# Three blocks of expert 0 ahead of the mixture of experts, four small blocks behind it, and routing in another order

## The chip, the cores and the metric

The kernel runs on one core of a Trainium2 chip. A core has TensorE (PE, matrix products; PEld is its weight load), VectorE (DVE), ScalarE (ACT), GpSimd (POOL) and SyncE (SP), which here only issues transfers; 16 DMA engines move the data between HBM and the on-chip memory. Each engine takes its instructions in order, and semaphores order the engines among each other. The metric is the time on the device of one execution, in microseconds (us), median of three runs.

## The reference

A trunk of two layers over 256 tokens of width 1024, in float32. The first layer (gating and pooling, then a dense SwiGLU) and the second layer's mixer (short convolution and latent attention) are not touched. The change lies at the end of the second layer's mixer, in the routing of its mixture of experts, and in the order of the experts' work:

```
x = x + g_m * mix
h = rmsnorm(x, norm_ffn_w) * (1 + sc_f) + sh_f
logits = h @ router_w                       # 256 tokens x 8 experts
top_v, top_i = top_k(logits, 2)             # two experts for each token
gates = softmax(top_v) put at top_i
y = sum over e of gates[:, e] * swiglu(h, w_gu[e], w_down[e])   # w_gu 1024 x 7168, w_down 3584 x 1024
out = x + g_f * y
```

All weights of all eight experts are read: 8 x 42 MiB, 336 transfers of 1 MiB.

## The kernel before

**Experts by place.** Routing counts the tokens of each expert. Expert 0 always has place 0. The other seven are put into places 1 to 7 by their counts, on the chip; places 1, 3 and 5 hold 128 tokens ("L"), places 0, 2, 4, 6 and 7 hold 64 ("S"). Which expert has a place from 1 up is known only when `Route.rest` has written `index` (L459); SP loads it into a register (L1519, in `Work.__init__`) and forms the addresses of that place's weights from it. Expert 0's addresses are known at compile time.

**Blocks.** The work of a place is cut into 7 blocks of 512 hidden columns. A block has four "up" chunks (1 MiB of `mgu` each) and two "down" chunks (1 MiB of `mdn` each). An S block multiplies the raw float32 weights (L1469 up, L1489 down). An L block first splits each chunk into a high and a low float32r part (ACT copy L113, DVE subtraction L116), and makes three products of them (L295, L297, L301). There are 35 S blocks and 21 L blocks. The list `blocks` mixes them: 2 S blocks (both of expert 0), then L blocks with the other S blocks spread between them, then 2 S blocks. In `seq` the up chunks of a block come before the down chunks of the block ahead of it. `run` emits one chunk of `seq`; `after(n, f)` puts a step n chunks later; `part_next` loads and splits an L chunk three L chunks ahead.

**Buffers.** A raw chunk lies in one of 14 buffers, taken in turn: `ring` (5), `keep` (8) and `extra` (1). An S chunk's buffer is free when PE has used it, an L chunk's when it has been split. `keep` and `extra` lie in memory that earlier phases give back; `extra` comes when the dense part is closed. All transfers are issued by SP.

**Orders.** The instructions of PE, ACT, DVE and POOL stand in program order from the end of the mixer on (`manual_schedule`). Those of SP are not in that set; a scheduler may put a transfer ahead of another.

**From the mixer to the experts.** `Close` finishes the mixer: `products(i, n)` are PE's last products for token half i and column half n, `add` the residual (DVE), `square` and `rstd` the norm (ACT, DVE, POOL). `flip` turns 512 columns of x (PE, copied by ACT), `use` multiplies them by the router (L1262). `Route.top2(i)` finds the two best experts of half i on DVE, `place(i)` counts positions within each expert by a product with a triangular matrix (L422, L425). `Gather.rows(i)` makes a selection matrix for half i (DVE, P and Q), `pick64(i)` applies it (PE L1363), `part64` scales the result into `hgS` (ACT and DVE); then the first up chunk of expert 0 can run. `gate_row` turns the last gate g_f into rows (8 transposes, L200). `rest` computes the softmax gates, the counts, the order of the experts, `index` and `over` (whether a place overflows).

**The end.** After the last S block `scatter2_front` multiplies the sum by g_f (L1494), `scatter2_back` spreads it to the tokens (PE L1501), adds it (DVE L1401) and stores four pieces of 256 KB (L1506, all from SP).

The order around the change, in the kernel before:

```python
cur = Gather(slots_of(stat, 0), 64, 4)
grows = [gate_row(1, 5, n, psa()) for n in range(2)]
cur.rows(0); route.top2(1); cur.pick64(0)
grow = gate_copy(pool, grows)
route.place(1); cur.rows(1); cur.pick64(1); cur.part64()
for n, ev in enumerate(seq):
    run(ev)
    if n == 1:
        placed, index, most, over = route.rest(pool, ranks, caps)
        ...
    if n == 5:
        gather_steps(1)
    if 7 <= n < 7 + AHEAD:
        part_next()
```

Of the kernel before, what the change touches and what calls it, by code (L numbers as in the profile page):

```python
# [7 lines left out]
F32 = mybir.dt.float32  # L8
# [13 lines left out]
NE = 8  # L22
# [20 lines left out]
def trunk_kernel(ctx, tc, x_in, c_in, pos_in, cols_in, rows_in,  # L43
# [345 lines left out]
    class Route:  # L389
# [12 lines left out]

        def top2(self, i, between=None):
            lg, m1, m2, f, oh1, oh2 = (t[:, i, :] for t in (self.lg, self.m1, self.m2, self.f, self.oh1, self.oh2))
            i1, i2, l2, maskb = (t[:, i, :] for t in (self.i1, self.i2, self.l2, self.maskb))
            vec.scalar_tensor_tensor(lg, self.lgp[i][:, :NE], self.ss[i][:, 3:4], shR, OP.mult, OP.add)
            vec.max_with_indices(m1, i1, lg)
            vec.tensor_copy(f[:, 0:1], i1[:, 0:1])
            vec.tensor_scalar(oh1, iota[:, :NE], f[:, 0:1], None, op0=OP.is_equal)
            vec.scalar_tensor_tensor(l2, oh1, -3.0e38, lg, OP.mult, OP.add)  # L410
            if between:
                between()
            vec.max_with_indices(m2, i2, l2)
            vec.tensor_copy(f[:, 1:2], i2[:, 0:1])
            vec.tensor_scalar(oh2, iota[:, :NE], f[:, 1:2], None, op0=OP.is_equal)
            vec.tensor_tensor(maskb, oh1, oh2, OP.add)
            vec.tensor_tensor(self.mask[:, i, :], oh1, oh2, OP.add)
# [8 lines left out]

        def rest(self, pool, ranks, caps):

# [9 lines left out]
            vec.tensor_tensor(self.gates, oh1, oh2, OP.add)  # L438
            ps = pst()
            pe.matmul(ps[:, 0:8], onesb, self.maskb[:, 0, :], start=True, stop=False)  # L440
            pe.matmul(ps[:, 0:8], onesb, self.maskb[:, 1, :], start=False, stop=True)
            vec.tensor_copy(self.count, ps[:, 0:8])

# [8 lines left out]
            vec.tensor_tensor(more, rank[:, None, :].to_broadcast([128, NE, NE]),  # L452
                              ranks[:, :, None].to_broadcast([128, NE, NE]), OP.is_equal)
            prod, placed = pool.tile([128, 8, NE, NE], F32, tag="w2", name="prod"), pl(8, NE)
            vec.tensor_tensor(prod, stat[:, :, None, :].to_broadcast([128, 8, NE, NE]),
                              more[:, None, :, :].to_broadcast([128, 8, NE, NE]), OP.mult)
            vec.tensor_reduce(placed, prod, AX.X, OP.add)
            index = pool.tile([128, NE], I32, name="index")
            vec.tensor_copy(index, placed[:, 7, :])  # L459

            above, most = pl(NE), pl(2)
# [406 lines left out]
    with Phase("mix1_late", w4=3, w2=2) as late, ExitStack() as early:  # L868
# [415 lines left out]
        flip(0, 1)  # L1284
        cl_.products(1, 1)
        cl_.add(1, 0)
        cl_.square(1, 0)
        use(0, 0)
        use(0, 1)
        flip(1, 0)  # L1290
        use(1, 0)
        cl_.add(1, 1)
        flip(1, 1)
        cl_.square(1, 1)
        route.top2(0, lambda: cl_.rstd(1))
        use(1, 1)
        route.place(0)
        early.close()
# [6 lines left out]
    shcol = mods[:, 1, 24:32]  # L1305
    with Phase("experts", w4=1, w2=2, aTL=1, hgH=1, hgL=1, hgS=1, P=1, Q=1, PT=3) as pool:
        sm = pool
# [184 lines left out]
        def scatter2_front(o):  # L1492
            og = sm.tile([128, 512], F32, tag="w2", name=nm("og"))
            vec.tensor_tensor(og, o, grow2, OP.mult)  # L1494
            return og

        def scatter2_back(gcol, og, g_, last=False):
            for i in range(2):
# [3 lines left out]
                for h in range(2):  # L1502
                    sl = slice(h * 512, (h + 1) * 512)
                    add_rows(i, h, ps[h], gcol[i])
                    if last:
                        sp.dma_start(out[i * 128:(i + 1) * 128, sl], ys[i][:, sl])  # L1506

# [21 lines left out]
        streams = {k: [(k, p, j) for p in range(NE) if (CAPS[p] == 128) == (k == "L") for j in range(7)] for k in "SL"}  # L1529
        blocks, nS, nL = [], len(streams["S"]), len(streams["L"])  # L1530
        for n in range(nL):
            while len(blocks) - n < 2 + (nS - 2) * n // nL:
                blocks.append(streams["S"][len(blocks) - n])
            blocks.append(streams["L"][n])
# [9 lines left out]
        parted = [ev for ev in seq if ev[0][0] == "L"]  # L1544
        AHEAD = 3
        halves, work, later = [], {}, []
# [108 lines left out]
        cur = Gather(slots_of(stat, 0), 64, 4)  # L1655
        grows = [gate_row(1, 5, n, psa()) for n in range(2)]
        cur.rows(0)
        route.top2(1)
        cur.pick64(0)
        grow = gate_copy(pool, grows)  # L1660
        route.place(1)
        cur.rows(1)
        cur.pick64(1)
        cur.part64()
        work[0] = Work(0, stat)
        work[0].g = cur
        for n, ev in enumerate(seq):
            run(ev)
            if n == 1:
                placed, index, most, over = route.rest(pool, ranks, caps)  # L1670
                cur.back()
                grow2 = pool.tile([128, 512], F32, name="grow2")
                for h in range(2):
                    act.copy(grow2[HALF[h]], grow[HALF[h], h * 512:(h + 1) * 512])
            if n == 5:
                gather_steps(1)
            if 7 <= n < 7 + AHEAD:
                part_next()
# [93 lines left out]
```

## Time and profile before

| | |
|---|---|
| median of 3 runs | 1303.78 us (1303.51 to 1304.12) |
| profiled execution, whole | 1305.34 us |
| its span, first to last instruction | 1303.5 us |
| mean granted TensorE clock | 0.973 of full |
| busy in the span: PE, DVE, ACT, POOL | 93%, 57%, 39%, 8% |
| DMA over the span | 358 GB/s |

Busy shares are of the span. A matmul's end is modelled, so a busy PE is not PE at its peak. The granted clock is 1.0 at 2.4 GHz and 0.5 at 1.2 GHz. Times of the trace count from the first instruction; the experts' first product starts at 444.78 us, the last one ends near 1292.5 us.

### The profile page before, as it was taken

What the parts mean: (1) busy time and instruction counts of PE and PEld (TensorE: products, weight loads), DVE (VectorE), ACT (ScalarE), POOL (GpSimd) and SP (SyncE); (2) the same over time, 40 slices, a digit from 0 to 9 for tenths busy, and PEclk for the clock granted to TensorE, in tenths of its full rate; (3) what the DMA queues carried; (4) which work ended last, traced back from release to release, by engine and by line L of the source; (5) the groups of instructions that cost most, each with busy time, mean ns of one, the idle gap of its engine ahead of it and who ended that gap; (6) DMA issues with size and microseconds to landing.
All of it is one profiled execution on the core that took longest, in us unless ns stands there. A gap on an engine that the chain in (4) does not pass through costs nothing.

```text
span 1303.5 us, 18766 instructions
## 1 busy us (share of the span) xinstructions
PE 1215.1 (93%) x7175; PEld 872.9 (67%) x7175; DVE 745.5 (57%) x1085; ACT 510.6 (39%) x768; POOL 108.3 (8%) x130
## 2 busy tenths in 40 slices
PE   1996999998999999999999999999999999999996
PEld 0575999997988766565565576665656666756663
DVE  3879898887786464353454445454535553544532
ACT  1044444345753254343353244343422353424420
POOL 2773000002171000000000000000000000000000
PEclk9997999999999799999999999999998999999999
DMA  6887888894667099999999998999999999999995
GB/s 264 341 315 293 285 351 329 322 358 163 225 220 266 10 421 421 418 420 419 419 420 418 419 419 348 419 419 419 420 418 421 403 394 419 419 418 419 419 419 203
DMA packets 65477, 466.47 MB, mean 358 GB/s; under 512 B 7522, under 2 KB 7650, under 8 KB 9315
## 3 DMA queue, kind: packets, MB, share of 16 engines
q1 hardware_dynamic: 65380, 465.20, 88.7%
q8 instruction: 58, 0.95, 0.3%
q14 instruction: 39, 0.32, 0.1%
HBM read 464.12 MB, written 1.05 MB: 357 GB/s over the span
## 4 chain that ended last, share of the span: by engine, by line
PE 69%; DMA 18%; DVE 7%; issue 2%; POOL 2%; ACT 2%; SPq 0%; DVEq 0%; POOLq 0%; ACTq 0%
PE gu L1469 14%; DMA raw<-in_mgu 13%; PE o L1489 7%; DMA raw<-in_mdn 5%; PE pb L314 3%; PE pb L313 3%; PE pb L316 3%; PE o L295 3%; PE o L297 3%; PE o L301 2%; PE g L295 2%; PE pa L599 2%; DVE junk L539 2%; PE u L295 2%; PE g L297 2%
## 5 line engine op out<-in xcount | busy, mean ns | idle before, releaser
L116 DVE TENSOR_TENSOR L<-raw,H 128x1024 fp32r<-128x1024 f32 x347 | 412.4, 1222 | 165.3 <-PE u L301 66.2
L113 ACT CAST H<-raw 128x1024 fp32r<-128x1024 f32 x350 | 350.7, 1046 | 119.8 <-PE u L297 80.1
L1469 PE MATMUL gu<-raw,hgS 128*64 128x256 f32 x2240 | 260.8, 386 | 10.3 <-DMA raw<-in_mgu 10.2
L1469 PEld LDWEIGHTS gu<-raw,hgS 128*64 128x64 f32 x2240 | 156.7, 138 | 105.8 <-DMA raw<-in_mgu 20.8
L1489 PE MATMUL o<-raw,aS 128*64 128x512 f32 x560 | 131.9, 605 | 1.7 <-DMA raw<-in_mdn 1.3
L539 DVE SCALAR_TENSOR_TENSOR junk<-raw,cact 128x1024 bf16<-128x1024 f32 x96 | 123.0, 1303 | 7.7 <-DMA raw<-in_ada 7.6
L1475 DVE TENSOR_TENSOR msg<-msg,gu 128x256 f32<-128x256 f32 x35 | 14.7, 421 | 192.7 <-ACT msg L1474 192.6
L313 PE MATMUL pb<-hH,H 128*128 128x256 f32 x432 | 106.3, 284 | 0.3 <-ACT cb L999 0.3
L314 PE MATMUL pb<-hL,H 128*128 128x256 f32 x432 | 106.0, 283 | 0.0
L1474 ACT ACTIVATE msg<-gu 128x256 f32<-128x256 f32 x35 | 13.4, 384 | 233.5 <-PE gu L1469 233.4
L313 PEld LDWEIGHTS pb<-hH,H 128*128 128x128 f32 x432 | 82.3, 190 | 1.1 <-ACT cb L999 0.6
L1489 PEld LDWEIGHTS o<-raw,aS 128*64 128x64 f32 x560 | 37.2, 138 | 68.1 <-issue 61.9
L314 PEld LDWEIGHTS pb<-hL,H 128*128 128x128 f32 x432 | 82.4, 191 | 0.4
L295 PE MATMUL g<-H,hgH 128*128 128x512 f32 x168 | 68.9, 410 | 0.0
L295 PE MATMUL u<-H,hgH 128*128 128x512 f32 x168 | 67.4, 401 | 0.0
L297 PE MATMUL g<-H,hgL 128*128 128x512 f32 x168 | 67.3, 401 | 0.0
L297 PE MATMUL u<-H,hgL 128*128 128x512 f32 x168 | 66.9, 398 | 0.0
L301 PE MATMUL u<-L,hgH 128*128 128x512 f32 x168 | 66.5, 396 | 0.0
L301 PE MATMUL g<-L,hgH 128*128 128x512 f32 x168 | 66.4, 395 | 0.0
L316 PE MATMUL pb<-hH,L 128*128 128x256 f32 x432 | 59.7, 280 | 0.0
L295 PE MATMUL o<-H,aTH 128*128 128x512 f32 x168 | 56.6, 418 | 0.0
L316 PEld LDWEIGHTS pb<-hH,L 128*128 128x128 f32 x432 | 54.9, 189 | 0.0
(396 smaller groups left out, 1528.1 us busy)
## 6 DMA issues: line engine op xcount, KB each, us to landing
raw<-in_mgu SPq DMA_DIRECT2D x224, 1024.0 KB, 19.8
raw<-in_mdn SPq DMA_DIRECT2D x112, 1024.0 KB, 19.8
raw<-in_ada SPq DMA_DIRECT2D x48, 1024.0 KB, 6.0
raw<-in_fgu SPq DMA_DIRECT2D x22, 1024.0 KB, 6.7
raw<-in_fdn SPq DMA_DIRECT2D x11, 1024.0 KB, 6.6
raw<-in_oin_c SPq DMA_DIRECT2D x6, 1024.0 KB, 5.1
raw<-in_ein_vp SPq DMA_DIRECT2D x4, 1024.0 KB, 7.8
raw<-in_eout SPq DMA_DIRECT2D x4, 1024.0 KB, 7.7
```

Of the source, the lines that this page charges most:

```text
L113: act.copy(self.to(q), raw[:, q * self.f:(q + 1) * self.f])
L116: eng.tensor_tensor(self.to(q), raw[:, q * self.f:(q + 1) * self.f], high.half(q).bitcast(F32), OP.subtract)
L295: pe.matmul(o, xH(k, i), wH(k, n), start=first and m == 0, stop=False)
L297: pe.matmul(o, xL(k, i), wH(k, n), start=False, stop=False)
L301: pe.matmul(o, xH(k, i), wL(k, n), start=False, stop=last and m == len(ks) - 1)
L313: pe.matmul(o, wH(k), hH[:, k, :], start=(k == 0), stop=False)
L314: pe.matmul(o, wH(k), hL[:, k, :], start=False, stop=False)
L316: pe.matmul(o, wL(k), hH[:, k, :], start=False, stop=(k == KD - 1))
L539: vec.scalar_tensor_tensor(junk, raw[:, a * D:(a + 1) * D], 1.0, cact, OP.mult, OP.mult, accum_out=mods[:, l, j + a:j + a + 1])
L599: pe.matmul(vp[part][i], h0[:, k, i * 128:(i + 1) * 128], w[:, kk * D + part * 512:kk * D + (part + 1) * 512], start=(k == 0), stop=(k == 7))
L1469: pe.matmul(gu[HALF[h], n * 256:(n + 1) * 256], g_.full[:, k, :], w[:, lo:lo + 256], start=(k == 0 and n == 0), stop=(k == KD - 1), skip_g ...
L1489: pe.matmul(o[HALF[h]], a[:, kk, c, :], w[:, kk * D + h * 512:kk * D + (h + 1) * 512], start=(j == 0 and c == 0 and kk == 0), stop=(j == 6 ...
```

## The change

1. **Blocks.** `LEAD` is 3: three S blocks of expert 0 stand ahead of the first L block (places 0.0, 0.1, 0.2), and four S blocks stand behind the last one. The L chunks begin to be loaded three chunks ahead of the first L chunk, that is at chunks 13 to 15 of `seq` in place of 7 to 9, and expert 1's gather begins at chunk 11 in place of 5.
2. **Routing.** `rest` is split: `counts` (two small products and a copy) runs before `pick64(1)`; `order` (the order of the experts, and of the table by place at first only the rows for count and index) runs behind the first chunk in place of the second; `gate` (the softmax gates) and the other six rows of the table come behind `index`.
3. **End of the mixer.** `products(1, 1)` is cut in two halves, the second behind `flip(1, 0)`; `top2(0)` and `place(0)` run whole before `add(1, 1)`, `flip(1, 1)`, `square(1, 1)` and `rstd(1)`, where `top2(0)` was interrupted for `rstd(1)`.
4. **Gate rows.** `gate_row` and its copies move behind chunks 1 and 2 of `seq`; the copy `grow2` goes, and `scatter2_front` multiplies two halves of 64 partitions by two instructions.
5. **Stores.** Of the four stores at the end SP issues two and ACT two.
6. A fourth buffer for `PT`.

```diff
-        def top2(self, i, between=None):
+        def top2(self, i):
...
-            if between:
-                between()
...
-        def rest(self, pool, ranks, caps):
+        def counts(self):
+            ps = psb("ps")
+            for i in range(2):
+                pe.matmul(ps[:, 0:8], onesb, self.maskb[:, i, :], start=(i == 0), stop=(i == 1))
+            vec.tensor_copy(self.count, ps[:, 0:8])
+
+        def gate(self):
...
-            ps = pst()
-            pe.matmul(ps[:, 0:8], onesb, self.maskb[:, 0, :], start=True, stop=False)
-            pe.matmul(ps[:, 0:8], onesb, self.maskb[:, 1, :], start=False, stop=True)
-            vec.tensor_copy(self.count, ps[:, 0:8])
+
+        def order(self, pool, ranks, caps):
...
-            vec.tensor_tensor(prod, stat[:, :, None, :].to_broadcast([128, 8, NE, NE]),
-                              more[:, None, :, :].to_broadcast([128, 8, NE, NE]), OP.mult)
-            vec.tensor_reduce(placed, prod, AX.X, OP.add)
-            index = pool.tile([128, NE], I32, name="index")
+
+            def by_place(lo, hi):
+                vec.tensor_tensor(prod[:, lo:hi], stat[:, lo:hi, None, :].to_broadcast([128, hi - lo, NE, NE]),
+                                  more[:, None, :, :].to_broadcast([128, hi - lo, NE, NE]), OP.mult)
+                vec.tensor_reduce(placed[:, lo:hi, :], prod[:, lo:hi], AX.X, OP.add)
+            by_place(6, 8)
             vec.tensor_copy(index, placed[:, 7, :])
-
+            self.gate()
+            by_place(0, 6)
...
-        cl_.products(1, 1)
+        cl_.products(1, 1, (0,))
         cl_.add(1, 0)
         cl_.square(1, 0)
         use(0, 0)
         use(0, 1)
         flip(1, 0)
+        cl_.products(1, 1, (1,))
+        route.top2(0)
         use(1, 0)
+        route.place(0)
         cl_.add(1, 1)
         flip(1, 1)
         cl_.square(1, 1)
-        route.top2(0, lambda: cl_.rstd(1))
+        cl_.rstd(1)
         use(1, 1)
-        route.place(0)
...
-            vec.tensor_tensor(og, o, grow2, OP.mult)
+            for h in range(2):
+                vec.tensor_tensor(og[HALF[h]], o[HALF[h]], grow[HALF[h], h * 512:(h + 1) * 512], OP.mult)
...
-                        sp.dma_start(out[i * 128:(i + 1) * 128, sl], ys[i][:, sl])
+                        (sp, act)[h].dma_start(out[i * 128:(i + 1) * 128, sl], ys[i][:, sl])
...
+        LEAD = 3
         for n in range(nL):
-            while len(blocks) - n < 2 + (nS - 2) * n // nL:
+            while len(blocks) - n < LEAD + (nS - LEAD - 2) * n // nL:
...
-        AHEAD = 3
+        AHEAD, FIRST = 3, seq.index(("LU", 1, 0, 0))
...
-        grows = [gate_row(1, 5, n, psa()) for n in range(2)]
         cur.rows(0)
+        cur.pick64(0)
         route.top2(1)
-        cur.pick64(0)
-        grow = gate_copy(pool, grows)
         route.place(1)
         cur.rows(1)
+        route.counts()
         cur.pick64(1)
...
+            if n == 0:
+                placed, index, most, over = route.order(pool, ranks, caps)
+                cur.back()
             if n == 1:
-                placed, index, most, over = route.rest(pool, ranks, caps)
-                cur.back()
-                grow2 = pool.tile([128, 512], F32, name="grow2")
-                for h in range(2):
-                    act.copy(grow2[HALF[h]], grow[HALF[h], h * 512:(h + 1) * 512])
-            if n == 5:
+                grows = [gate_row(1, 5, m, psb()) for m in range(2)]
+            if n == 2:
+                grow = gate_copy(pool, grows)
+            if n == FIRST - 5:
                 gather_steps(1)
-            if 7 <= n < 7 + AHEAD:
+            if FIRST - 3 <= n < FIRST - 3 + AHEAD:
                 part_next()
```

## Rows read from the trace of the kernel before

**Rows 1.** Page, part 2: busy tenths of the DMA engines, 40 slices of 32.6 us

```profile
DMA  6887888894667099999999998999999999999995
```

**Rows 2.** Waits of SP's queue, 416 to 456 us: us in total, times, longest

```profile
SPq L1519 <- DVE pl L466: 37.6, 1, 37.6
```

**Rows 3.** Transfers issued from 380 to 432 us: count, size, us to landing

```profile
raw<-in_mgu SPq DMA_DIRECT2D x8, 1024.0 KB, 7.0
...
raw<-in_mdn SPq DMA_DIRECT2D x1, 1024.0 KB, 4.8
```

**Rows 4.** Windows: length, busy by engine, granted clock, DMA share, GB/s

```profile
422.00:424.00 2.00, 2.00 (x14) 1.77 (x13) 0.99 (x3) 0.94 (x3) 0.55 (x1) 1.00 0.68 287
424.00:426.00 2.00, 2.00 (x10) 1.58 (x9) 0.55 (x1) 1.37 (x4) 0.00 (x0) 1.00 0.00 0
...
480.00:500.00 20.00, 18.35 (x114) 10.59 (x113) 7.43 (x8) 7.26 (x10) 0.00 (x0) 1.00 1.01 419
```

**Rows 5.** Timeline, 434 to 454 us: start, us, engine, line, operation

```profile
434.74 1.95 PE L200 MATMUL pa<-ident,mods 128*128 128x128 f32 x8
...
436.56 3.65 PE L1363 MATMUL pt<-Q,x 128*128 128x64 f32 x16
...
441.17 3.68 PE L1363 MATMUL pt<-Q,x 128*128 128x64 f32 x16 [0.93 <-DVE Q L1337]
...
444.78 4.76 PE L1469 MATMUL gu<-raw,hgS 128*64 128x256 f32 x32
...
449.91 0.17 DVE L447 SCALAR_TENSOR_TENSOR pl<-stat,iota 128x8 f32<-128x8 f32 x1
...
452.53 0.17 DVE L459 CAST index<-pl 128x8 int32<-128x8 f32 x1
...
453.75 0.36 SPq L86 DMA_DIRECT2D raw<-in_mgu  x1
```

**Rows 6.** Waits of PE, 455 to 600 us

```profile
PE gu L1469 <- DMA raw<-in_mgu: 6.6, 13, 0.6
PE o L1489 <- DMA raw<-in_mdn: 0.6, 1, 0.6
```

**Rows 7.** Waits of PE, 455 us to the end

```profile
PE gu L1469 <- DMA raw<-in_mgu: 10.2, 20, 0.6
...
PE o L1489 <- DMA raw<-in_mdn: 1.3, 2, 0.6
```

**Rows 8.** Timeline of PE: two down chunks and four up chunks, S blocks

```profile
837.36 3.65 PE L1489 MATMUL o<-raw,aS 128*64 128x512 f32 x16
...
841.53 7.13 PE L1469 MATMUL gu<-raw,hgS 128*64 128x256 f32 x64
```

**Rows 9.** A window of the middle, and the stretch ahead of the experts

```profile
800.00:820.00 20.00, 19.16 (x132) 12.17 (x132) 7.97 (x9) 4.75 (x6) 0.00 (x0) 1.00 0.75 299
...
430.00:447.00 17.00, 15.34 (x74) 13.53 (x75) 7.03 (x38) 3.87 (x10) 1.69 (x27) 0.50 0.01 1
```

**Rows 10.** Timeline at the end of the mixer, 427 to 434 us

```profile
427.53 0.69 DVE L345 TENSOR_TENSOR x<-x,res 128x512 f32<-128x512 f32 x1
...
428.56 0.23 DVE L406 SCALAR_TENSOR_TENSOR lg<-lg,ss,shR 128x8 f32<-128x8 f32 x1 [0.34 <-PE lg L1262]
...
431.07 1.09 PE L1248 MATMUL pt<-ident,x 128*128 128x128 f32 x4
...
432.90 1.88 PE L1262 MATMUL lg<-aR,xT 128*128 128x8 f32 x8 [0.73 <-ACT xT L1256]
```

**Rows 11.** Timeline at the end of the run

```profile
1285.40 7.09 PE L1489 MATMUL o<-raw,aS 128*64 128x512 f32 x32
...
1292.53 0.69 DVE L1494 TENSOR_TENSOR og<-o,grow 128x512 f32<-128x512 f32 x1 [7.56 <-PE o L1489]
...
1295.22 2.70 SPq L1506 DMA_DIRECT2D out<-y  x4
1295.77 1.40 DVE L1401 SCALAR_TENSOR_TENSOR y<-pa,pl,y 128x512 f32<-128x512 f32 x2
```

More of the change, by code (lines that the diff above doesn't have):

```diff
@@ L453, in rest @@
                               ranks[:, :, None].to_broadcast([128, NE, NE]), OP.is_equal)
+            index = pool.tile([128, NE], I32, name="index")
             prod, placed = pool.tile([128, 8, NE, NE], F32, tag="w2", name="prod"), pl(8, NE)
-            vec.tensor_tensor(prod, stat[:, :, None, :].to_broadcast([128, 8, NE, NE]),
-                              more[:, None, :, :].to_broadcast([128, 8, NE, NE]), OP.mult)
-            vec.tensor_reduce(placed, prod, AX.X, OP.add)
-            index = pool.tile([128, NE], I32, name="index")
+            def by_place(lo, hi):
[3 more added lines that the diff above has]
+            by_place(6, 8)
             vec.tensor_copy(index, placed[:, 7, :])
+            self.gate()
+            by_place(0, 6)
             above, most = pl(NE), pl(2)
@@ L1305, in trunk_kernel @@
     shcol = mods[:, 1, 24:32]
-    with Phase("experts", w4=1, w2=2, aTL=1, hgH=1, hgL=1, hgS=1, P=1, Q=1, PT=3) as pool:
+    with Phase("experts", w4=1, w2=2, aTL=1, hgH=1, hgL=1, hgS=1, P=1, Q=1, PT=4) as pool:
         sm = pool
```

## The prediction

> **What bounds the kernel now.** I read the page's slices first: the DMA engines are full from the fifteenth slice to the end, with one dent in the middle, and there is a hole just ahead of that [rows 1]. From 600 us on that looks like a kernel bound by its weights: 336 transfers of 1 MiB, each 2.50 us at the 419 GB/s of an undisturbed window [rows 4], 840 us in all. The second look goes to the hole. Nine expert transfers are issued up to 416 us [rows 3]; their bytes have landed by 424 us, and the next window is empty [rows 4]. SP sits 37.6 us in one wait [rows 2]: it wants the register with the expert of place 1, and `index` is written at 452.53 [rows 5]. The next transfer goes out at 453.75, so 1.05 us pass from the end of the index write to the first weight that depends on it, and the DMA engines stand for some 30 us.
>
> The third look is at who waits afterwards, since a full DMA doesn't say that PE starves. An S block's up chunk takes PE 7.13 / 4 = 1.78 us and a down chunk 1.82 us [rows 8], against 2.50 us for its transfer; so PE outruns the transfers in S blocks and is overtaken in L blocks. Where PE waits for a chunk it therefore loses 2.50 - 1.78 = 0.72 us. PE waits for weights 14 times up to 600 us [rows 6] and 22 times up to the end [rows 7], so 8 times in the 700 us behind the first stretch. The shown idle, 7.2 us in the first stretch, is less than 14 x 0.72 = 10.1 us, because matmul ends are modelled; I go by the 10.1. Elsewhere it is the other way round: in the window at 800 us the transfers ran at a share of 0.75 of the time against 1.01 elsewhere, 5 us lost to full buffers [rows 9]. So this phase is nearly balanced, paced by PE over most of it and by the transfers where S blocks stand close together. A saved microsecond of transfers is worth something only where PE waits.
>
> **The change, part by part.**
>
> *Blocks in front and index first.* Ahead of the first chunk with an unknown expert there now stand chunks 0 to 13, 14 transfers of expert 0, as many as there are buffers. Five more than the nine can be in flight in the hole: 5 x 2.50 = 12.5 us. If SP still meets its wait after fewer of them (the register load is emitted at chunk 11, so after 12), it is 3 x 2.50 = 7.5 us. The index comes sooner too. Before, the chain from L447 to `index` ran from 449.91 to 452.70, 2.8 us, behind two chunks of PE work [rows 5]; now the counts are there before the second pick, and the chain can start when the scaling is done, about 446 us, with a table of a quarter of the size. I take 448.9 us at SP against 453.75: 4.9 us. Head start together 17.4 us (12.4 with 12 transfers). Up to 600 us PE lost 10.1 us to late weights, so either size covers it: **-10.1**. The rest of the head start runs into full buffers. The 8 waits after 600 us I leave: transfers that full buffers have stopped, as at 800 us, have no head start left, since it is cut back to the same 14 buffers. Bounds for this part: half of it (-5) and all 22 waits (-15.8).
>
> *Four S blocks at the end.* The sum of PE's work is unchanged. In the kernel before, the last 32 matmuls ran without a gap from 1285.40 to 1292.53 [rows 11], so PE was behind the transfers there, and four S blocks only shift its slack. **0**; the other end is a rival below.
>
> *Routing and the end of the mixer.* `top2(0)` can start when `use(0, 1)` is done; before, that was 428.56 [rows 10]. With half of `products(1, 1)` behind it, it starts some 1.4 us earlier (an estimate: half its products); its dozen steps of about 0.2 us take 2.5 us. But `add(1, 1)` now stands behind it and behind `place(0)` on DVE. It ended at 428.2 [rows 10]; now it ends near 431.5, and `flip(1, 1)`, `square`, `rstd` and `use(1, 1)` wait for it. `flip(1, 1)` began at 431.07 before [rows 10], since it stood behind `use(1, 0)`, so it is only 0 to 1 us later. The selection for half 0 needs memory that `use(1, 1)` gives free and comes where it came, then `pick64(0)`, `top2(1)`, `place(1)`, `rows(1)`, `pick64(1)`: both picks of 3.65 us stand in one chain with the second top-2, and nothing of it is taken out. The 8 transposes of `gate_row` that stood ahead of `pick64(0)` (1.95 us at the low clock [rows 5]) filled PE's wait for Q. First product at 444.8 as before: **0**, bounds +1.1 and -3.7 (both picks at the full clock, a rival).
>
> *Gate rows.* The same 8 transposes now stand in the stream of chunks. At the full clock they are worth half of 1.95: **+1.0** (bound 1.95). The copies go to ACT, which is not late there; without that cover they would cost two copies. Two small matmuls of the counts leave the stream; I count nothing for them.
>
> *Two instructions in place of one for the last multiplication by g_f.* DVE takes 0.69 for 128 partitions [rows 11]; half the partitions should take as long. In four of five scatters two chunks of PE work cover it. In the last one PE's first product needs the first half only, and the additions that follow go at 0.70 each whatever comes first: **0**, bound +0.7.
>
> *Stores.* The last addition ends at 1297.17, SP's last issue at 1297.92 [rows 11]; two queues can take some 0.3 of that away: **-0.3**, bounds -1.4 (if the four transfers ran side by side) and +0.7. The Trainium skill (DMA: Bandwidth & Descriptors, Issuing engines are not separate DMA queues) says that transfers from several engines run on the same 16 DMA engines and that only issue time is saved. By that rule the sum stays with -0.3, not -1.4; no run here shows a second queue.
>
> The fourth `PT` buffer frees no wait that the trace shows: 0. Sum: -10.1 + 1.0 - 0.3 = -9.4. The profiled execution took 1305.34 us (span 1303.5 and 1.84 around it); that makes 1295.9 for it, and 1303.78 - 9.4 = **1294.4 us** for the median, which lies 1.6 us below the profiled one.
>
> **The rivals.**
>
> *A. The transfers are the pace after all.* For it: the row of nines [rows 1]. Then the whole head start comes back: 1303.78 - 17.4 + 1.0 - 0.3 = 1287.1. Against it: PE waits for weights in no more than 22 places [rows 7], and the transfers themselves stop at 800 us [rows 9].
>
> *B. The four S blocks at the end are paced by transfers.* Between the first and the last L block there are now 31 - 3 = 28 S blocks in place of 31, so more of PE's time is L there and SP waits longer for buffers. The last four S blocks need 24 transfers, 60 us, and PE 4 x (7.13 + 3.65) + 1 for transposes = 44 us. If a of the 24 have landed when PE gets there, PE loses 16 - 2.5a us: 1 us at a = 6, 8.5 at a = 3 (1302.9). Below a = 2.6 the gain of 9.4 is gone, and at a = 0 it is 1294.4 + 16 = 1310.4, slower than before. For it: PE is the faster one in S blocks by 0.72 us a chunk. Against it: PE had 7 us of work in hand behind the last weights before [rows 11], and 14 buffers hold more than 6 chunks.
>
> *C. The clock stays high in front.* Before, PE stood still a few times between small products near 429 us, and the granted clock was 0.50 (1.2 GHz) from 430 to 447 us [rows 9]. The new order puts 1.4 us of large products between `flip(1, 0)` and `use(1, 0)`. If the clock holds, two picks take 1.8 in place of 3.65 us: 1294.4 - 3.7 = 1290.7. The Trainium skill (TensorE: Matmul & The Clock Gate, What's actually happening) has the clock follow how busy PE has been; by that rule a better filled stretch can keep it. Against it: PE waits for the delayed `add(1, 1)` between `place(0)` and `flip(1, 1)`, about 1.5 us, and for Q afterwards.
>
> *D. Half the gain.* SP's scheduler keeps the wait for the register ahead of most of the 14, or the start slips by 1 us: 1299 to 1302.
>
> **How the numbers follow.** A difference of 0.2% is 2.6 us, about what a measurement here can tell from none. Chances: the forecast 0.58, A 0.16, C 0.10, B 0.12 (half of it within 2.6 us of before, half slower), D 0.04 (half of it faster). Faster: 0.58 + 0.16 + 0.10 + 0.02 = 0.86; same: 0.06 + 0.02 = 0.08; slower: 0.06. Low end: -15.8 in place of -10.1 and about half of C's 3.7, 1286, which also takes in most of A. High end: 5 us of the early waits stay and 0.6 are lost at the start or at the gate rows, 1300. Beyond these lie B, D and the last part of A.
>
> **What the profile after would show.** The index written near 448 us, 12 to 14 expert transfers issued before it, the hole of the DMA engines shorter by more than half. No wait of PE for weights up to 600 us, but more windows with the DMA share below 1.01, which is the head start lost to full buffers. `add(1, 1)` ending near 431.5, the first product of expert 0 near 444.8. At the end two issues from ACT and an end of PE's work near 1283. I am wrong if PE still waits for weights early (then the head start didn't come), if it waits some ten times in the last four S blocks (B), or if PE's stream itself got slower: a longer stretch at the low clock or new waits at gathers and scatters.

## The result and the profile after

Five runs of the changed kernel took 1283.88 to 1288.47 us, median **1286.9**; five runs of the kernel before beside them 1303.51 to 1306.19, median 1304.12. The ratio is 0.9863 [0.9847, 0.988]: faster by 17.2 us. The forecast was 1294.4 in a range of 1286 to 1300, so the side and the range held, but the gain is 1.8 times the 9.4 us of the sum. In a second set of runs (e2 below) it is 20.0 us.

The profiled execution has a span of 1285.1 us against 1303.5, 18.4 less. Its DMA slices (page, part 2, 32.1 us each) answer to [rows 1]: the empty slice ahead of the row of nines now reads 7, and the one dent in the middle is still there.

```profile
DMA  6978799895554799999999998999999999999996
```

SP's longest wait from 416 to 456 us (total, times, longest) is still the one for the expert's number, but 16.6 us in place of 37.6 [rows 2], and before it 14 expert transfers have been issued (second fence, 380 to 448 us: count, size, median time to landing) in place of nine [rows 3]:

```profile
SPq L1529 <- DVE d L435: 16.6, 1, 16.6
```

```profile
raw<-in_mgu SPq DMA_DIRECT2D x12, 1024.0 KB, 9.0
raw<-in_mdn SPq DMA_DIRECT2D x2, 1024.0 KB, 18.7
```

The timeline around the start of the experts (start, length, engine, line, operation, in brackets the idle time before and what ended it) answers to [rows 5, 10]. `add(1, 1)` ends at 432.70, 4.5 us later than before; counted from the step of `rstd(0)` near 423 us, which itself came 1.3 later, that is 3.2, where the forecast had 3.3; `flip(1, 1)` stands 1.67 us for it; both picks still take 3.65 and 3.68; the first product comes at 446.54; `index` is written 3 us sooner than before, at 449.55, and the first weight that needs it goes out at 450.78.

```profile
432.01 0.69 DVE L345 TENSOR_TENSOR x<-x,res 128x512 f32<-128x512 f32 x1
432.85 1.08 PE L1255 MATMUL pt<-ident,x 128*128 128x128 f32 x4 [1.67 <-DVE x L345]
...
442.94 3.68 PE L1372 MATMUL pt<-Q,x 128*128 128x64 f32 x16 [0.88 <-DVE Q L1346]
...
446.54 3.34 PE L1478 MATMUL gu<-raw,hgS 128*64 128x256 f32 x16
...
449.55 0.17 DVE L465 CAST index<-pl 128x8 int32<-128x8 f32 x1
...
450.78 0.36 SPq L86 DMA_DIRECT2D raw<-in_mgu  x1
...
452.06 1.09 PE L200 MATMUL pb<-ident,mods 128*128 128x128 f32 x8
```

PE's waits from 455 us to the last scatter (us in all, times, longest):

```profile
PE pt L1354 <- DVE Q L1346: 3.6, 2, 1.8
PE pt L1463 <- ACT oH L319: 3.0, 2, 1.5
PE pt L1511 <- DVE y L1410: 3.0, 4, 0.8
PE gu L1478 <- DMA raw<-in_mgu: 2.9, 6, 0.5
...
PE o L1498 <- DMA raw<-in_mdn: 0.7, 1, 0.7
```

Seven waits for weights are left of 22 [rows 7], and none of them lies ahead of 600 us, where there were 14 [rows 6]. At 0.72 us each that is 10.8 us. But the stretch from the first product to the last `og` shrank from 847.75 us (444.78 to 1292.53, [rows 5, 11]) to 827.29 (446.54 to 1273.83): 20.5 us. So about half of the gain isn't in these waits.

The other half shows in the windows (length, busy of PE, PEld, DVE, ACT and POOL, granted clock, DMA share, GB/s). Before, beyond those of [rows 4, 9]:

```profile
620.00:640.00 20.00, 18.41 (x70) 11.52 (x68) 11.90 (x13) 8.07 (x9) 0.00 (x0) 0.91 1.01 420
700.00:720.00 20.00, 18.13 (x93) 11.72 (x91) 12.93 (x22) 8.06 (x12) 0.00 (x0) 0.91 1.01 419
...
978.00:979.00 1.00, 1.00 (x3) 0.54 (x4) 0.56 (x1) 0.00 (x0) 0.00 (x0) 1.00 1.05 434
...
980.00:981.00 1.00, 1.00 (x3) 0.81 (x4) 0.64 (x1) 0.00 (x0) 0.00 (x0) 0.50 0.97 401
```

After:

```profile
620.00:640.00 20.00, 20.00 (x122) 12.84 (x121) 10.26 (x11) 7.43 (x9) 0.00 (x0) 1.00 1.01 420
...
780.00:800.00 20.00, 19.16 (x115) 10.51 (x114) 9.83 (x13) 5.47 (x8) 0.00 (x0) 1.00 0.77 318
...
980.00:1000.00 20.00, 18.29 (x122) 11.84 (x120) 10.54 (x13) 5.99 (x8) 0.00 (x0) 1.00 1.01 419
...
699.00:700.00 1.00, 1.00 (x6) 1.00 (x6) 1.00 (x2) 0.00 (x0) 0.00 (x0) 0.50 1.02 426
```

A window of 20 us at a mean of 0.91 has lost 0.09 x 20 = 1.8 us of full clock. In windows of 1 us these are single stretches at 1.2 GHz (0.50), worth 1.7 us each. Before has six between 455 us and the last product, beginning at 627, 709, 737, 979, 993 and 1020 us; after has one, at 698. Five stretches fewer are 8.5 us. What PE did ahead of one of them stands in the timeline of before: it waited 1.59 us at a small scatter, and the products behind it then took 0.79 and 0.63 us in place of about 0.40.

```profile
977.95 1.90 PE L1501 MATMUL pt<-og,PT 64*128 64x512 f32 x4 [1.59 <-DVE y L1401]
...
979.78 0.79 PE L295 MATMUL g<-H,hgH 128*128 128x512 f32 x1
...
980.37 0.63 PE L295 MATMUL u<-H,hgH 128*128 128x512 f32 x1
```

All six of before begin within about two microseconds of the end of such a standstill: two at small scatters (1.6 us), two at large gathers (1.8), two at large scatters (1.5), and these six are the only waits of PE of 1.5 us or more in that stretch. After has four of them (the two at small scatters fell to 0.8 us), and one low stretch. The 14 profiled executions of this document show 52 such standstills in that stretch, 26 of them followed by a low stretch, and no low stretch there that does not follow one. The profiled pair then closes: weights -10.8, clock -8.5, shorter waits at small scatters -1.9 (4.9 to 3.0 us in all), gate rows +1.1, later start +1.8, end +0.3: -18.0 against the -18.4 of the spans.

The end, on the timeline, answers to [rows 11]; `og` in two halves takes 0.70 each, and the four stores go out from two queues.

```profile
1273.83 1.41 DVE L1504 TENSOR_TENSOR og<-o,grow 64x512 f32<-64x512 f32 x2 [7.56 <-PE o L1498]
...
1276.51 2.34 SPq L1516 DMA_DIRECT2D out<-y  x2
...
1277.30 1.65 ACTq L1516 DMA_DIRECT2D out<-y  x2
```

### The profile page after: what moved, and what is told of

It is laid out like the page before. It is cut to its first block, busy times and chain, and to the rows that moved or that the text cites. A ratio compares the mean times of both kernels' runs of the same rounds, so it can differ in the third digit from the quotient of the medians.

```text
span 1285.1 us, 18770 instructions
## 1 busy us (share of the span) xinstructions
PE 1203.1 (94%) x7175; PEld 870.8 (68%) x7175; DVE 748.5 (58%) x1092; ACT 508.6 (40%) x766; POOL 107.3 (8%) x130
## 4 chain that ended last, share of the span: by engine, by line
PE 74%; DMA 9%; DVE 7%; POOL 4%; issue 3%; ACT 2%; SPq 0%; POOLq 0%; DVEq 0%; ACTq 0%
PE gu L1478 16%; PE o L1498 8%; DMA raw<-in_mgu 5%; DMA raw<-in_mdn 4%; PE pb L316 3%; PE pb L314 3%; PE pb L313 3%; PE o L295 3%; PE o L297 3%; PE g L295 3%; PE o L301 3%; PE u L297 3%; PE u L295 3%; PE g L297 3%; PE g L301 3%
## 5 line engine op out<-in xcount | busy, mean ns | idle before, releaser
L1478 PE MATMUL gu<-raw,hgS 128*64 128x256 f32 x2240 | 255.3, 383 | 3.1 <-DMA raw<-in_mgu 2.9
L1484 DVE TENSOR_TENSOR msg<-msg,gu 128x256 f32<-128x256 f32 x35 | 14.7, 421 | 197.5 <-ACT msg L1483 197.4
```

The lines of the kernel that those rows point to most:

```text
L1478: pe.matmul(gu[HALF[h], n * 256:(n + 1) * 256], g_.full[:, k, :], w[:, lo:lo + 256], start=(k == 0 and n == 0), stop=(k == KD - 1), skip_g ...
L1484: vec.tensor_tensor(sg, sg, u, OP.mult)
```

## The experiments

Two theories stood against each other. **Head start:** the gain is the early waits for weights that the third block in front takes away, plus what the clock gives back; the end and the stores are worth nothing. **End:** the four S blocks at the end carry a good part of it. A third one came in on the way, **standstills:** what PE loses in the middle hangs on waits of 1.5 us and more at gathers and scatters, through the clock. In the table the ratio is to the runs of before that stood beside each kernel, P is the time from the first product of expert 0 to the last `og`, and the counts are those of the one profiled execution: waits of PE for weights (in brackets those up to 600 us), other waits of 1.5 us or more from 455 us on, and stretches at 1.2 GHz between 455 us and the last product (one of double length counts as two).

| kernel | median us | ratio to before, 95% | weights | 1.5 us or more | low | P us |
|---|---|---|---|---|---|---|
| before | 1304.1 | | 22 (14) | 6 | 6 | 847.8 |
| after | 1286.9 | [0.9847, 0.988] | 7 (0) | 4 | 1 | 827.3 |
| before again (e1) | 1303.9 | [0.9982, 1.0019] | 24 (14) | 6 | 4 | 847.9 |
| after again (e2) | 1284.6 | [0.9827, 0.9874] | 7 (0) | 4 | 0 | 826.9 |
| old blocks (e4) | 1296.8 | [0.9918, 0.9959] | 15 (5) | 6 | 4 | 841.7 |
| blocks alone (e5) | 1288.5 | [0.9861, 0.9908] | 10 (0) | 4 | 2 | 830.0 |
| 3 in front, 2 at end (e6) | 1283.9 | [0.9825, 0.9873] | 4 (0) | 4 | 1 | 824.9 |
| 2 in front, 4 at end (e7) | 1296.7 | [0.9929, 0.9967] | 19 (6) | 4 | 3 | 839.1 |
| other front (e8) | 1282.7 | [0.9814, 0.9863] | 7 (0) | 4 | 1 | 827.4 |
| old blocks, split (e9) | 1291.9 | [0.9885, 0.9919] | 24 (5) | 2 | 1 | 835.9 |
| one store queue (e10) | 1285.3 | [0.9833, 0.9863] | 7 (0) | 4 | 3 | 830.5 |
| e8 and split (e11) | 1275.4 | [0.9764, 0.9796] | 10 (0) | 2 | 0 | 820.9 |
| same, 2 at end (e12) | 1278.8 | [0.9782, 0.9817] | 15 (0) | 1 | 1 | 825.1 |
| same, 4 in front (e13) | 1274.6 | [0.9747, 0.9786] | 12 (0) | 1 | 0 | 820.5 |

For the ten profiles that keep the steps at gathers and scatters where before has them (all but e9 and e11 to e13), P less 0.72 us for each wait for weights and 1.7 us for each low stretch lies between 819.4 and 824.1 us, while P itself runs from 824.9 to 847.9. These two terms carry most of the difference between the kernels.

### Both kernels again (e1, e2)

Both unchanged, to see how far the numbers repeat.

> The kernel before once more, for the clock of each of its executions. Three theories share the 17 us. Head start: PE's 14 early waits for weights (10 us) are gone, the rest is unsettled. Clock: some 8 us more come from stretches of about 4 us at 1.2 GHz, five in the middle of before, one in after. End: the four small blocks behind the last L block let PE catch up, worth some 8 us. If the clock's part is chance from execution to execution, the spans of this kernel spread by several us and follow the mean granted clock (0.001 of clock is 1.3 us of span). If it belongs to the order of the work, all executions lie within 2 us at a clock of 0.972 to 0.974. Time 1304 by all theories.

> The changed kernel once more, for the clock of each execution. Seen so far: spans of 1282.0 to 1286.6 at clocks of 0.980 to 0.975. Chance: the same spread again, span following clock by 1 to 1.3 us for each 0.001. Head start and end say nothing of the spread. Time 1284 to 1289.

Measured: 1303.94 (1298.44 to 1306.91, 12 runs) and 1284.55 (1283.21 to 1285.91), the latter 20.0 us below the 1304.59 of before beside it. The waits for weights repeat, 24 with 14 early, and 7 with none; the low stretches don't: four of the same six places, and none in place of one. The executions of one kernel also differ by this: of e1, those with a mean granted clock of 0.979 took a span of 1296.6 and 1297.3 us, those with 0.973 took 1304.0 to 1305.0. The 0.006 are worth 0.006 x 1300 = 7.8 us, about the whole difference. So the profiled pair overstates the clock: (1 - mean clock) x span, averaged over executions, is 32.7 us for e1 (12) and 26.8 for after (5 and 5 of e2), which makes the clock's share of the gain some 5.9 us, not 8.5. It is not exact: the first five executions of after lose 28.5 us and those of e2 25.1.

### The block order taken back (e4)

```
-        LEAD = 3
+        LEAD = 2
...
-            while len(blocks) - n < LEAD + (nS - LEAD - 2) * n // nL:
+            while len(blocks) - n < LEAD + (nS - LEAD) * n // nL:
```

> The changed kernel with the old order of blocks (two S blocks in front, two behind); all else of the change stays. Head start: the index is some 3 us earlier against the start, but no more than ten transfers of expert 0 can go out ahead of it, so 5 to 6 us of the 10 us of early waits stay away and about half of the waits remain: 1298 to 1300. Clock and end, if they belong to the blocks: nothing further, five low stretches in the middle as before. Clock, if it belongs to the routing or the gate rows: 1290 to 1292.

Measured: 1296.78, 7.8 us below before and some 10 to 12 above after, so between the two forecasts. The rest of the change, with the index at 447.27 us, brings the early waits from 14 to 5, but all six standstills are back, and low stretches with them, two single ones and one of double length. PE's waits, 455 us to the end:

```profile
PE gu L1478 <- DMA raw<-in_mgu: 6.7, 13, 0.6
PE pt L1511 <- DVE y L1410: 5.1, 4, 1.7
...
PE o L1498 <- DMA raw<-in_mdn: 1.3, 2, 0.6
```

### The blocks alone (e5)

The kernel before with the new block order, and with what the blocks need: the fourth `PT` buffer, and for its room `og` in two halves without `grow2`; the new block order without these deadlocks and gave no time (e3). Routing, gate rows and stores as before.

```
-            while len(blocks) - n < 2 + (nS - 2) * n // nL:
+            while len(blocks) - n < LEAD + (nS - LEAD - 2) * n // nL:
...
-            if n == 5:
+            if n == FIRST - 5:
```

> The new order of blocks in the kernel before, as in the one that did not build, with the fourth PT buffer and the last multiplication in two halves (without grow2), which it needs to fit; routing, mixer end, gate rows and stores as before, so the index still comes near 453. Head start: 12.5 us of it by five more transfers, no early wait of PE for weights, 1304 - 10 = 1294. Clock by the order of blocks: small scatters now fall beside S chunks where DVE is not busy splitting, PE's waits for them shrink from 1.6 to 0.8 us and at most one low stretch is left in the middle (each costs 1.7 us of full clock, four to six of them before): another 7 to 9 us, 1285 to 1287, the whole gain. If the routing is needed for the gain: 1292 or more.

Measured: 1288.53 against 1303.21 beside it, -14.7, which lies between the 1294 without a gain of the clock and the 1285 to 1287 with it. The index comes as late as before, at 452.70, and still no wait for weights is left up to 600 us. So either cure works on the same waits: the third block takes away all 14 by itself, the earlier index 9 of them (e4). Together (17.2 and 20.0 us) they aren't worth the sum of the two, 14.7 + 7.8. Averaged over its executions e5 lost 29.8 us of full clock, before beside it 31.4: on average the new blocks alone gave back 1.6 us of clock, less than its profiled execution suggests.

```profile
452.70 0.17 DVE L459 CAST index<-pl 128x8 int32<-128x8 f32 x1
```

### Front and end apart (e6, e7)

e6 keeps three blocks in front and has two at the end (first diff), e7 has two in front and four at the end (second).

```
-            while len(blocks) - n < LEAD + (nS - LEAD - 2) * n // nL:
+            while len(blocks) - n < LEAD + (nS - LEAD) * n // nL:
```

```
-        LEAD = 3
+        LEAD = 2
```

> The changed kernel with three S blocks in front but two at the end (the other S blocks spread over the middle as before). Head start: the same as the changed kernel, 1285. End: PE is 2 blocks of S behind the weights as before, 1285 + 4 to 8 us. Clock: it depends on where the small scatters now fall; one to three low stretches, 1285 to 1290.

> The changed kernel with two S blocks in front but four at the end. Head start: as with the old order of blocks, no more than ten transfers ahead of the index, some five early waits left, 3 to 4 us lost against the changed kernel: 1288 to 1289. End: 1285 to 1286, the front not needed. Clock: low stretches as the scatters fall, zero to three of them, 1.7 us each.

Measured: 1283.86 and 1296.71. Four blocks at the end without the third in front are no better than the old order (1296.78, e4); the third block without them is as fast as after. The theory of the end falls for these kernels; e12 comes back to it. The forecast of the head start for e7, 1288 to 1289, missed too: against after, e7 has 12 more waits for weights, six of them behind 600 us, and two more low stretches, 12 x 0.72 + 2 x 1.7 = 12.0 us, where its P is 11.8 longer. So the third block spares later waits as well; with two blocks at the end it is the same, ten late waits in e4 and four in e6. PE's waits in e6, from 440 us on:

```profile
PE pt L1511 <- DVE y L1410: 4.2, 4, 1.7
...
PE o L1498 <- DMA raw<-in_mdn: 1.4, 3, 0.6
...
PE gu L1478 <- DMA raw<-in_mgu: 0.5, 1, 0.5
```

and in e7, from 440 us on:

```profile
PE gu L1478 <- DMA raw<-in_mgu: 7.0, 14, 0.6
...
PE o L1498 <- DMA raw<-in_mdn: 3.0, 5, 0.7
```

### Another order at the end of the mixer (e8)

`add(1, 1)` goes ahead of `top2(0)`, which waits for `use(1, 0)` again; `place(0)` comes last.

```
-        route.top2(0)
-        use(1, 0)
-        route.place(0)
         cl_.add(1, 1)
         flip(1, 1)
         cl_.square(1, 1)
+        use(1, 0)
+        route.top2(0)
         cl_.rstd(1)
         use(1, 1)
+        route.place(0)
```

> The changed kernel with another order at the end of the mixer: products(1, 1) in one piece, add(1, 1) directly behind add(1, 0), flip(1, 1) directly behind flip(1, 0), then use(1, 0), the whole top2(0), rstd(1), use(1, 1), place(0). In the changed kernel flip(1, 1) stands still for 1.7 us until add(1, 1), which waits behind top2(0) and place(0) on DVE, and each step after it follows from that. If the start of the experts sets the end (PE paced from there): the first product comes 3 us sooner and the time is 1281 to 1282. If the transfers set the end: the start comes sooner and the time stays at 1285. If the low clock in front only moves: start 1 us sooner, 1284.

Measured: 1282.73 [0.9814, 0.9863]; after stood at 1286.9 and 1284.55. On the timeline of e8, `flip(1, 1)` no longer stands still, and the experts begin 19.08 us after the step of `rstd(0)` shown first (425.19 to 444.27); in after it is 22.47 (424.07 to 446.54), in the other six profiles with its front (e2, e4, e6, e7, e9, e10) 21.35 to 21.94, and P is that of after to 0.1 us. So the start comes 2.3 to 3.4 us sooner and the median falls by 1.8 to 4.2: what is won at the start isn't lost behind it, and the order that the change chose costs some 2 to 3 us there.

```profile
425.19 0.55 POOL L358 TENSOR_TENSOR ss<-ss,nhalf 128x1 f32<-128x1 f32 x1 [19.20 <-DVE ss L357]
...
430.72 1.07 PE L1255 MATMUL pt<-ident,x 128*128 128x128 f32 x8
...
444.27 3.37 PE L1477 MATMUL gu<-raw,hgS 128*64 128x256 f32 x16
```

### One queue for the stores (e10)

```
-                        (sp, act)[h].dma_start(out[i * 128:(i + 1) * 128, sl], ys[i][:, sl])
+                        sp.dma_start(out[i * 128:(i + 1) * 128, sl], ys[i][:, sl])
```

> The changed kernel with all four stores at the end issued by SP. By issue time alone: the distance from the last addition's start to the end of the span grows by 0.3 us, not to be told apart in the median (1284 to 1286). If the two queues moved the four pieces side by side: 1 us or more.

Measured: 1285.27 (1284.38 to 1289.09), between the two results of after. From the start of the last `og` to the end of the span it takes 1287.2 - 1276.08 = 11.1 us. But this distance scatters whatever the queues: 9.7 to 11.4 us in the ten profiles with two (11.3 in after and in e2, 9.8 in e8), 10.5 to 11.4 in the four with one (before, e1, e5, e10). A gain from the second queue isn't shown, and one of some tenths isn't excluded. Here three low stretches came with the block order of after, which had one and none: part of them is chance. The end of e10:

```profile
1276.08 1.41 DVE L1504 TENSOR_TENSOR og<-o,grow 64x512 f32<-64x512 f32 x2 [7.56 <-PE o L1498]
...
1278.75 2.79 SPq L1516 DMA_DIRECT2D out<-y  x4
```

### The standstills taken out (e9)

On the old blocks of e4, the two halves of a small scatter go one chunk apart, and the picks of a large gather come one chunk later, so that Q and y are there when PE comes.

```
-                after(2, lambda: scatter2_back(w_.gcol, og, w_.g))
+                after(2, lambda: scatter2_back(w_.gcol, og, w_.g, halves=(0,)))
+                after(3, lambda: scatter2_back(w_.gcol, og, w_.g, halves=(1,)))
...
-                    after((1, 1, 3, 4)[n], lambda n=n: w_.g.pick(n))
+                    after((2, 2, 4, 5)[n], lambda n=n: w_.g.pick(n))
```

> The changed kernel with the old order of blocks (1296.8), and with the steps moved in which PE stood still: the two token halves of a small scatter one chunk apart (PE waited 0.8 to 1.6 us for DVE between them), a large gather's picks one chunk later (PE waited 1.8 us for Q). So far PE's time from the first product to the last sum is 820 to 824 us plus 0.72 us for each wait for weights plus 1.7 us for each stretch at 1.2 GHz. If the low stretches follow PE's standstills: four of them go to at most one, 5 us, and with 6 us of standstill less PE meets the weights more often; 1288 to 1292. If they are chance: still three or four, 1292 to 1296.

Measured: 1291.87, 4.9 us below e4. The rows for y and for Q at large gathers are gone from PE's waits, two of six standstills are left, and one low stretch of four. Nine more waits for weights came in their place (24, from 15), which fits a PE that reaches the chunks sooner. PE's waits from 440 us on:

```profile
PE gu L1478 <- DMA raw<-in_mgu: 10.9, 21, 0.6
...
PE o L1498 <- DMA raw<-in_mdn: 1.9, 3, 0.6
```

P fell by 5.8 us: 9 x 0.72 = 6.5 lost to weights, 8.7 us of shown standstills (5.1 and 3.6) and 3 x 1.7 = 5.1 of clock won make -7.3. Two of the three low stretches that went (the double one counts as two) lay behind a step that was moved; the third, at 730 us in e4, lay behind a standstill at a large scatter that stayed, so not all of the clock is owed to the moved steps. Averaged over executions e9 lost 24.5 us of full clock, e4 29.0.

### All of it together (e11, e12, e13)

e11 is after with the front of e8, the split of e9, and the gate rows ahead of the first pick, where PE waits anyway; e12 has two blocks at the end, e13 four in front. Against e8:

```
         cur = Gather(slots_of(stat, 0), 64, 4)
+        grows = [gate_row(1, 5, n, psa()) for n in range(2)]
         cur.rows(0)
...
         route.top2(1)
+        grow = gate_copy(pool, grows)
         route.place(1)
```

> The changed kernel with the mixer end of the run front2 (1282.7), gate_row's transposes back ahead of the first pick where PE waits for Q, and the scatter and gather steps moved as in e9. If the sum of PE's parts holds: 1282.7 - 1.1 for the transposes - up to 6 for the standstills, with some of that given back to waits for weights: 1277 to 1280. If the transfers take it all back: 1281 to 1283.

> The same with two S blocks at the end in place of four (three in front). The end theory fell with e6 and e7; if the number of blocks at the end is worth nothing, this lies within 2 us of e11; if PE runs into the weights more often with four at the end, as e6 with 4 waits against 7 suggests, it is 1 to 3 us faster: 1275 to 1279.

> The kernel of e11 (1275.4, 10 waits of PE for weights, 7 of them behind 600 us) with four S blocks of expert 0 in front in place of three, four at the end as there. With three blocks the 14 transfers ahead of the first unknown expert are as many as there are buffers. If what counts is that the buffers can be filled before the index is known: a fourth block adds nothing, 1274 to 1278 with 8 to 13 waits. If it is the number of S blocks in front itself (two to three was worth 12 us with the old steps): 3 us or more faster, 1272 or less, and fewer waits. If S blocks in front only let PE run into the transfers sooner: 1278 or more, and new waits up to 600 us.

Measured: 1275.39, 1278.84 and 1274.58: e11 is 9.2 and 11.5 us below the two results of the change, and e13, the fastest of all, 30 below the 1304.82 of before beside it. e11 begins at 439.40 us, 7.1 sooner than after, 3.6 of them behind `rstd(0)`, where the change is (18.88 us to the first product), and its P is 6.4 shorter; e12 and e13, with the same front, begin at 440.73 and 443.23. e12 missed both forecasts: it is 3.5 us slower than e11, with 15 waits for weights in place of 10. With most of the standstills gone, four blocks at the end are worth something after all. PE's waits in e12, from 455 us on:

```profile
PE gu L1477 <- DMA raw<-in_mgu: 6.3, 12, 0.6
...
PE o L1497 <- DMA raw<-in_mdn: 1.9, 3, 0.6
```

A fourth block in front adds nothing that these runs can tell, as forecast (12 waits): with 14 buffers, no more than 14 of its chunks can be in flight. With P at 820.5 to 825 the waits for weights rise again (10 to 15). In e12 and e13, as in e6 and e9, the DMA share is 0.95 or more in every window of 10 us from 460 to 1250 us, where before falls to 0.59 in the one from 810 and after to 0.52 in the one from 790. There the transfers hardly stop, so little is left to be had on PE's side without touching the transfers.

## Why the prediction was right, and where its size was off

- **Early waits, -10.1: right.** They went from 14 to 0; e4 and e5 show that the third block does it alone and the index most of it. The head start was a little smaller than reckoned (five more transfers, and the first one behind the wait at 450.78, in e2 at 448.71, where 448.9 was forecast), which cost nothing: it was more than was needed, as the prediction had it. Of the 8 later waits it left alone, 7 remained. Its reason for leaving them alone, that full buffers leave no head start, doesn't hold for every order: the third block takes the late waits from 10 to 4 with two blocks at the end (e4, e6) and from 13 to 7 with four (e7, after).
- **Four blocks at the end, 0: right,** by e6 and e7, though not for every order (e12 is 3.5 us slower than e11). Rival B falls: the changed kernel has no wait for weights in its last four S blocks. In e7, e11 and e13 there are four, three and three.
- **Start, 0: right.** Counted from the same step of `rstd(0)` the first product comes after 21.8 to 22.2 us in the three profiles with the old front (before, e1, e5) and after 21.4 to 22.5 in the seven with the new one. In the profiled pair it is 22.00 and 22.47; the rest of the 1.8 on the clock of the span lies upstream of the change. The price of `add(1, 1)` behind `top2(0)` was seen in `flip(1, 1)`; that the old order was not the best of the bounds is shown by e8.
- **Rival C fell:** both picks ran at 1.2 GHz as before. The low stretch lies at 432 to 450 us in after, and PE waits in it for `add(1, 1)` and for Q, as was argued against the rival.
- **Gate rows, +1.0:** 1.09. **`og` in halves, 0:** 0.70 each, covered as said.
- **Stores, -0.3: not shown.** The last issue ends 5.1 us after `og` began, against 5.4, so the issue did come 0.3 sooner; at the end of the span, which scatters by 1.7 us, that can't be told (e10). The Trainium skill (DMA: Bandwidth & Descriptors, Issuing engines are not separate DMA queues) allows no more than the issue time. These runs neither confirm nor refute that.
- **Rival A** names almost the measured time, 1287.1, but not the cause. If the transfers set the pace, the stretch with all DMA engines full would have held to the end; after has a window from 780 to 800 us with a share of 0.77 (shown above), and e9 gained 4.9 us by taking away waits of PE that have nothing to do with weights.
- **Rival D fell:** 14 transfers were out before the wait for the register, and no early wait was left.
- **The step that was off in size: a term that the sum lacked,** PE's own stream. The prediction took the time between waits for weights as given ("the sum of PE's work is unchanged") and looked at the clock only in front. The mean granted clock of the kernel before, 0.973, is 0.027 x 1303.5 = 35.2 us of lost full clock in all; the stretch from 429 to 447 us holds 8.5 of it, and a search through the windows would have shown six separate stretches of 1.7 us behind 455 us, each behind a standstill at a gather or a scatter. The change moves these. In the profiled pair they are -8.5 us, over all executions some -5.9, with 1.9 more from shorter waits at the small scatters. With the terms as measured (15 waits for weights -10.8, gate rows +1.1, clock -5.9, small scatters -1.9; start and end at 0) the sum is -17.5, against -17.2 and -20.0 in the two sets of runs. The closeness is partly luck, since the clock's share is known to no better than a few us.

What stays open: how much of the clock's share belongs to the block order, how much to the rest of the change and how much to chance. Averaged over executions the new blocks alone gave back 1.6 us (e5), and the rest of the change without them 3.2 (e4, 29.0 lost against 32.2 beside it). With two blocks in front and standstills left in (before, e1, e4, e7) 16 of 22 standstills were followed by a low stretch (one in e4 by a double one, from 972 to 980 us); with three (after, e2, e5, e6, e8, e10) 8 of 24. That the waits for weights nearby make a low stretch likelier would fit, but no run varied them alone.

## What to carry to other kernels

A transfer that must wait for a computed index wants as many known transfers ahead of it as there are buffers; an earlier index and more work in front cure the same waits. Here the work in front took away all 14 of the early ones and some later ones, the earlier index nine, and both together gained less than their sum. Before an order of blocks is changed, walk through the granted clock window by window: behind a standstill of 1.5 us as much again was lost to the clock in 26 of 52 cases here, and an order that moves gathers and scatters to shorter waits can win both. Where PE and the transfers are nearly balanced, each gain on one side turns partly into waits on the other.

## What was not expected of the hardware

Six standstills of 1.5 to 1.8 us in the middle of a stretch that PE otherwise fills were each followed by a stretch at 1.2 GHz that lost 1.7 us; in the other profiled execution of the same kernel the same six standstills had four low stretches behind them, and its spans run from 1296.6 us at a mean clock of 0.979 to 1305.0 at 0.973. The Trainium skill (TensorE: Matmul & The Clock Gate, What's actually happening) has the clock throttled by default and released by activity, varying from run to run, and puts the ramp at under 1% of a typical span. The variation agrees with the traces. The figure is for a ramp; here the six stretches come to 6 x 1.7 = 10.2 us, 0.8% of 1303.5, and all the full clock lost in that execution to 35.2 us, 2.7%. The 10.2 alone are more than half of what this change gained.
